# A decoder layer's input projection by Strassen's seven block products, in two sweeps over the contraction

## The chip, the core and the metric

The kernel runs on one core of a Trainium2 chip, as one launch. The metric is the device time of that launch in microseconds; lower is better. Five engines work side by side, each through its own list of instructions in order: TensorE (PE, matrix products), VectorE (DVE), ScalarE (ACT), GpSimd (POOL) and SyncE (SP), which here only issues transfers. They wait for each other by semaphores.

## What is computed

The reference, cut to what matters (S = 1024 positions, model width 2048, 8 heads of 128):

```python
h = jnp.einsum('bsd,de->bse', x, w_in[layer])           # 2048 -> 6144 columns
q, k, v, u_pool, gate = jnp.split(h, [1024, 2048, 3072, 4096], axis=-1)
q, k = rotary_partial(q, positions), rotary_partial(k, positions)   # first 32 of 128
attn = dilated_attention_mixture(q, k, v)               # three strides, one softmax
pooled = [causal_pool_minus_identity(u_groups[g], POOL_WINDOWS[g]) for g in range(4)]
pool_out = einsum(pooled, w_pool[layer]) * pool_scale[layer]
y = concatenate([attn, pool_out]) * silu(gate)
out = jnp.einsum('bse,ed->bsd', y, w_out[layer])
x = layer_norm(DEEPNORM_ALPHA * x + out, ln_gain, ln_bias)
```

The input projection is a product of 1024 x 2048 by 2048 x 6144 in float32.

## The kernel before, in words

**Products.** TensorE takes float32 operands here in a shortened form (F32R). So each operand is split into a high part (a copy by ACT into F32R) and a low part (source minus high part, by DVE): `split`, lines 107 to 109. A product is then three matmuls, high by high, high by low and low by high, summed in PSUM.

**Input projection** (lines 237 to 289). x, transposed, lies split in SBUF for the whole stage: 16 tiles of 128 x 1024 for each part. The 6144 columns are 48 blocks of 128, taken in an order written out in `rounds` (lines 186 to 195): q, k, v and gate of a head, then the next head, at the end the pooling inputs and their gates. Per block the loop runs over 16 contraction tiles; each gives three products by two halves of 512 positions, six matmuls (line 640). The v blocks are computed with positions on the partitions, so that they need no transpose: 12 matmuls of 256 columns per contraction tile (line 633). Weights come in pieces of 128 x 512 (`Pieces`, line 111), three loaded and four split ahead; such a piece holds four contraction tiles of a block.

**Background.** Everything else of the stage (rotation, scores, exponentials, transposes, values, pooling) is cut into steps that wait in a queue, `Background` (line 33). After each block's contraction tile, `bg.tick()` (line 643) adds 0.70 to a credit, 1.0 in the last 12 rounds, and runs a step for each whole credit; so steps are laid into the PE's list between products. `bg.drain(tag)` runs steps at once up to a tag, where a later block needs their buffers. `bg.later` puts off a store by some ticks, so that SP does not stand waiting for it. Rotation (`qk_evac`, line 249) works on the PSUM banks themselves: shuffle and two products, one on DVE and one on POOL (line 265), a sum, then the split. v goes through DRAM once to be read back by residue (`v_d`). Pooling windows (`u_evac`) and their projections (`pool_project`, line 502 the matmul) are background steps too.

**Output projection** (lines 734 to 807). Gated outputs are stored to DRAM (`y_d`), loaded back, split, and multiplied with w_out (`mm3`, line 731), four banks at a time. The first y tiles and weights are loaded and split during the last block of the input projection (lines 613 to 616). Norm and stores of finished rows are background steps again; the last row block is a short tail behind the last matmul.

## Time and profile before

| | us |
|---|---|
| three runs | 1565.33, 1565.43, 1565.63 |
| median | 1565.43 |
| span of the profiled execution (first to last instruction) | 1564.2 |
| PE busy in it | 1551.0 |
| DVE / ACT / POOL busy | 631.6 / 446.2 / 54.6 |
| transfers | 149.75 MB, mean 96 GB/s |

The profiled execution's own time beside its span is not listed; its span lies 1.2 us below the median of the runs. A profile is read here in this order: which engine is busy, which chain of work ended last, what each stage of the span looks like, and last what a single instruction takes. A matmul's own duration overlaps with the next one's, so its cost is the distance of starts.

### The profile page before, as it was taken

To read this page: it belongs to the slowest core of one execution; us is meant where nothing else is said; L and a number is where in the kernel's file an instruction comes from. 1 tells how busy PE (TensorE), PEld (TensorE's weight loads), DVE (VectorE), ACT (ScalarE), POOL (GpSimd) and SP (SyncE) were. 2 spreads that over 40 slices of the span, in tenths; PEclk is the share of its full clock that TensorE was granted. 3 is DMA by queue.
4 is the path that set the end of the run, shared out by engine and by line. 5 is a ranking of instruction groups with operands and counts; after the bars stand their busy time and mean duration, and the time that the engine had idled before them with its cause. 6 is when DMAs were issued, how large, how long until landed. Compare 5 with 4: busy or idle time off the path is not lost.

```text
span 1564.2 us, 20097 instructions
## 1 busy us (share of the span) xinstructions
PE 1551.0 (99%) x8116; PEld 1308.5 (84%) x8116; DVE 631.6 (40%) x1155; ACT 446.2 (29%) x788; POOL 54.6 (3%) x59
## 2 busy tenths in 40 slices
PE   9999999999999999999999999999999999999997
PEld 7898889888899888998888888888888888888886
DVE  4362433233441434424342113454153435476446
ACT  4333232142431323323323113222132424222310
POOL 0010100001000000000000000000000000000001
PEclk9999999999999999999999999999999999999999
DMA  7431213311124111241111222222213557357512
GB/s 239 146 110 34 61 41 89 107 35 41 54 68 128 41 41 54 60 117 57 38 54 54 68 75 84 97 75 61 61 54 114 167 205 242 115 197 242 146 52 104
DMA packets 73085, 149.75 MB, mean 96 GB/s; under 512 B 8288, under 2 KB 12256, under 8 KB 71712
## 3 DMA queue, kind: packets, MB, share of 16 engines
q1 hardware_dynamic: 72704, 148.19, 30.6%
q8 instruction: 63, 1.03, 0.3%
q10 hardware_dynamic: 288, 0.29, 0.1%
q14 instruction: 30, 0.25, 0.1%
HBM read 126.42 MB, written 22.02 MB: 95 GB/s over the span
## 4 chain that ended last, share of the span: by engine, by line
PE 98%; DVE 1%; ACT 1%; issue 0%; DMA 0%; DVEq 0%; SPq 0%
PE mm_ps L640 54%; PE mm_ps L731 10%; PE mm_ps L633 10%; PE s_ps L731 6%; PE o_ps L731 3%; PE t_ps L731 3%; PE s_ps L633 1%; PE s_ps L502 1%; PE s_ps L320 1%; PE o_ps L381 1%; PE o_ps L396 1%; PE s_ps L327 1%; PE o_ps L640 1%; PE o_ps L397 1%; PE t_ps L640 1%; PE t_ps L368 0%
## 5 line engine op out<-in xcount | busy, mean ns | idle before, releaser
L109 DVE TENSOR_TENSOR w_lo<-w_raw,w_hi 128x512 fp32r<-128x512 f32 (+1 forms) x337 | 234.3, 696 | 643.8 <-ACT w_hi L108 643.7
L108 ACT ACTIVATE w_hi<-w_raw 128x512 fp32r<-128x512 f32 (+1 forms) x337 | 212.0, 630 | 806.0 <-PE mm_ps L640 426.3
L640 PE MATMUL mm_ps<-h,w_hi 128*128 128x512 f32 x1248 | 395.9, 398 | 0.0
L640 PE MATMUL mm_ps<-l,w_hi 128*128 128x512 f32 x1248 | 386.1, 391 | 0.0
L640 PE MATMUL mm_ps<-h,w_lo 128*128 128x512 f32 x1248 | 386.0, 390 | 0.0
L640 PEld LDWEIGHTS mm_ps<-h,w_lo 128*128 128x128 f32 x1248 | 234.6, 188 | 50.3
L640 PEld LDWEIGHTS mm_ps<-l,w_hi 128*128 128x128 f32 x1248 | 234.5, 188 | 50.0
L640 PEld LDWEIGHTS mm_ps<-h,w_hi 128*128 128x128 f32 x1248 | 225.6, 188 | 45.7 <-issue 4.0
L633 PE MATMUL mm_ps<-w_hi,h 128*128 128x256 f32 x448 | 128.3, 286 | 0.0
L633 PE MATMUL mm_ps<-w_hi,l 128*128 128x256 f32 x448 | 126.8, 283 | 0.0
L633 PE MATMUL mm_ps<-w_lo,h 128*128 128x256 f32 x448 | 126.7, 283 | 0.0
L633 PEld LDWEIGHTS mm_ps<-w_hi,h 128*128 128x128 f32 x448 | 85.9, 192 | 0.5
L633 PEld LDWEIGHTS mm_ps<-w_lo,h 128*128 128x128 f32 x448 | 85.9, 192 | 0.1
L633 PEld LDWEIGHTS mm_ps<-w_hi,l 128*128 128x128 f32 x448 | 85.8, 192 | 0.0
L731 PE MATMUL mm_ps<-w_hi,h 128*128 128x512 f32 x192 | 74.7, 389 | 0.0
L731 PE MATMUL mm_ps<-w_lo,h 128*128 128x512 f32 x192 | 74.7, 389 | 0.0
L731 PE MATMUL mm_ps<-w_hi,l 128*128 128x512 f32 x192 | 74.7, 389 | 0.0
L731 PE MATMUL s_ps<-w_hi,h 128*128 128x512 f32 x128 | 49.8, 389 | 0.0
L731 PE MATMUL s_ps<-w_lo,h 128*128 128x512 f32 x128 | 49.8, 389 | 0.0
L731 PE MATMUL s_ps<-w_hi,l 128*128 128x512 f32 x128 | 49.8, 389 | 0.0
L342 ACT ACTIVATE p_t<-p_t,nm 128x128 f32<-128x128 f32 (+3 forms) x64 | 35.9, 562 | 32.1 <-DVE nm L335 31.7
L333 DVE CUSTOM_DVE_ANT_0 p_t<-s_ps,mask 128x128 f32<-128x128 f32 (+3 forms) x64 | 31.4, 490 | 28.1 <-PE s_ps L327 25.7
(176 smaller groups left out, 1704.7 us busy)
## 6 DMA issues: line engine op xcount, KB each, us to landing
w_raw<-in_w_in_dram SPq DMA_DIRECT2D x159, 256.0 KB, 2.7
w_raw<-in_w_out_dram SPq DMA_DIRECT2D x112, 256.0 KB, 2.7
w_raw<-in_w_v_dram SPq DMA_DIRECT2D x64, 256.0 KB, 2.7
z<-in_x_n_dram SPq DMA_DIRECT2D x8, 1024.0 KB, 5.1
p_t<-in_x_t_dram SPq DMA_DIRECT2D x15, 512.0 KB, 5.4
out_dram<-z SPq DMA_DIRECT2D x30, 256.0 KB, 3.4
y_d<-p_t SPq DMA_DIRECT2D x8, 512.0 KB, 3.8
y_d<-v_f SPq DMA_DIRECT2D x8, 512.0 KB, 3.5
```

The lines of the kernel that those rows point to most:

```text
L108: ACT.activation(hi, src, AF.Copy)
L109: DVE.tensor_tensor(out=lo, in0=src, in1=hi, op=ALU.subtract)
L320: PE.matmul(s[e][:, n - 2 * P:n], a[:, b * P:b * P + P], k[:, b * P - P:b * P + P], start=j == 0, stop=j == 2)
L327: PE.matmul(s[e][NF * r:NF * r + NF, :width(b) - 2 * P], qf[:, q0:q0 + NF], kv[:, :b - 1, r, :], start=True, stop=True, tile_position=(0, ...
L333: DVE.tensor_tensor_reduce(out=pt, in0=s[e][:, :n], in1=mask[:, NM - n:], op0=ALU.add, op1=ALU.max, scale=1.0, scalar=-3.0e38, accum_out=mx)
L342: ACT.activation(pt, pt, AF.Exp, scale=SCALE, bias=st.pop(("m", m, e)), accum_out=den)
L381: PE.matmul(o[:, 0:2 * P], v[:, 2 * m], p[:, 1:3], start=True, stop=False)
L396: PE.matmul(ov[:, e], v[:, 0, r], far_t[0][:, :, c], start=True, stop=False)
L397: PE.matmul(ov[:, e, 4:6], v[0:64, 1, r], far_t[1][:, :, c], start=False, stop=True)
L633: PE.matmul(o, x[kc][:, ss], y[:, es], start=kc == 0 and n == 0 and b % 2 == 0, stop=kc == KC - 1 and n == 2 and b % 2 == 1)
L640: PE.matmul(t[f], a[:, es], b[kc][:, c], start=kc == 0 and n == 0, stop=kc == KC - 1 and n == 2)
L731: PE.matmul(o, a[:, k % 2, ss], b, start=k == 0 and n == 0, stop=k == KC - 1 and n == 2)
```

## The change

The 48 column blocks are taken in 24 pairs, and the contraction in two sweeps of 1024. In a sweep, positions (two halves of 512), contraction (two quarters of 512) and the two blocks of a pair form 2 x 2 blocks, and the pair's four results come from seven block products in place of eight, with sums and differences of x quarters (made once per sweep, `combo`) and of weight quarters (made per pair on POOL, `combine`) as operands. A block product is 12 matmuls of 512 columns. The first sweep runs over all pairs with no background steps and stores the four results of a pair to DRAM (`q_d`); the second loads them back and adds its own. v now comes out with its columns on the partitions and is transposed by PE (`values`). Rotation works in SBUF. Gates, pooling inputs and window means go through DRAM (`g_d`, `u_d`, `m_d`). The pool projections run after the last pair, and the output projection's buffers are opened after them.

The diff, cut to its core:

```diff
-Q0, K0, U0, G0 = 0, 8, 16, 24
 NF = 32
 NM = 6 * NF + 2 * P
+PAIRS = []
+for _h in range(NH):
+    if _h < 4:
+        PAIRS.append(("u", _h))
+    elif _h in (5, 7):
+        PAIRS.append(("p", (_h - 5) // 2))
+    PAIRS += [("qk", _h), ("vg", _h)]
+PAIRS += [("p", 2), ("p", 3)]
+NP = len(PAIRS)
...
+    def gate(self, key):
+        self.steps.append((None, key))
+    def _blocked(self):
+        while self.steps and self.steps[0][0] is None:
+            if self.steps[0][1] not in self.ready:
+                return True
+            self.steps.popleft()
+        return not self.steps
...
             return
         self.credit += self.rate
-        while self.credit >= 1.0 and self.steps:
+        while self.credit >= 1.0 and not self._blocked():
             self.credit -= 1.0
             self.steps.popleft()[0]()
     def drain(self, tag=None):
...
+        if tag is not None and all(t != tag or f is None for f, t in self.steps):
             return
-        while self.steps:
+        while not self._blocked():
             fn, t = self.steps.popleft()
             fn()
...
+    bg = Background(0.55)
...
+        def cut(self, t):
+            hi = wp.tile([P, 512], F32R, name="w_hi", bufs=3)
+            lo = wp.tile([P, 512], F32R, name="w_lo", bufs=3)
+            split(hi, lo, t)
             self.ready.append((hi, lo))
-            self.made = 1
...
+        def combine(self, n, k):
+            if n >= len(self.order):
+                return
+            r, s = self.raw, self.s
+            a, b, op = {1: (r.get((n, 2)), r.get((n, 3)), ALU.add),
+                        2: (s.get((n, 1)), r.get((n, 0)), ALU.subtract),
+                        3: (r.get((n, 0)), r.get((n, 2)), ALU.subtract),
+                        4: (r.get((n, 1)), s.get((n, 2)), ALU.subtract)}[k]
+            t = wp.tile([P, 512], F32, name="w_sum", bufs=3)
+            POOL.tensor_tensor(out=t, in0=a, in1=b, op=op)
+            s[n, k] = t
...
+                lambda: (self.load(n + 1, 0, 2), self.cut(r[n, 0]), self.combine(n, 2)),
+                lambda: (self.cut(s[n, 2]), self.combine(n, 3)),
+                lambda: self.cut(r[n, 1]),
+                lambda: (self.cut(s[n, 3]), self.load(n + 1, 3, 1)),
+                lambda: (self.cut(s[n, 1]), self.combine(n, 4)),
+                lambda: self.cut(r[n, 3]),
+                lambda: (self.cut(s[n, 4]), self.combine(n + 1, 1)),
+            ]
+        def step(self):
+            if self.steps:
+                self.steps.popleft()()
...
+    def combo(i, src, cuts=1):
+        hi = cp.tile([P, 4, 512], F32R, name=f"ch{i}")
+        lo = cp.tile([P, 4, 512], F32R, name=f"cl{i}")
+        combos[i] = (hi, lo)
+        n = 4 // cuts
+        for c in range(cuts):
+            split(hi[:, c * n:c * n + n], lo[:, c * n:c * n + n], src[:, c * n:c * n + n])
...
+    def product(i, o, first, last):
+        wh, wl = weights.take()
+        xh, xl = combos[i]
+        for kc in range(4):
+            es = slice(kc * P, kc * P + P)
+            for n, (a, b) in enumerate(((wh, xh), (wh, xl), (wl, xh))):
+                PE.matmul(o, a[:, es], b[:, kc], start=first and kc == 0 and n == 0,
+                          stop=kc == 3 and n == 2, skip_group_check=True)
+            if kc == 1:
+                weights.step()
+            bg.tick()
...
+    def quarter():
+        return wp.tile([P, 512], F32, name="q4", bufs=5)
...
+    def store_q(pair, q, t, ticks=2):
+        bg.later(lambda: SP.dma_start(q_d[pair][q], t), ticks)
...
+        a = bank()
+        do(1, a, True)
+        x = temp()
+        ACT.activation(x, a, AF.Copy)
+        b = bank()
+        evac("x", x)
+        do(6, b, True)
+        u2 = temp()
+        add(DVE, u2, x, b)
+        evac("u2", u2)
+        do(2, a, False)
+        evac(0, a, None)
+        do(7, b, False)
+        u3 = temp()
+        add(DVE, u3, x, b)
+        evac("u3", u3)
+        c = bank()
+        do(5, c, True)
+        evac(3, c, u3)
+        do(4, b, False)
+        evac(2, b, x)
+        do(3, c, False)
+        evac(1, c, u2)
+    weights.load(0, 0)
+    x_load(0, 0, 0, cuts=4)
+    weights.load(0, 1)
+    x_load(0, 1, 0, cuts=2)
+    weights.load(0, 2, 3)
...
+    ready = {
+        1: lambda: combo(1, xr[0, 0], 4),
+        2: lambda: combo(2, xr[1, 0], 2),
+        3: lambda: combo(3, xr[1, 1], 2),
+        7: lambda: (x_sum(DVE, "t1", xr[0, 1], xr[0, 0]),
+                    x_sum(POOL, "t3", xr[1, 1], xr[0, 1], xr[0, 1]), combo(7, xr["t3"])),
+        5: lambda: (combo(5, xr["t1"]), x_sum(DVE, "t2", xr[1, 1], xr["t1"])),
+        6: lambda: (combo(6, xr["t2"]), x_sum(DVE, "t4", xr[1, 0], xr["t2"])),
+        4: lambda: combo(4, xr["t4"]),
+    }
+    first_pair(0, ready)
...
+    def sums_out(pair):
+        def evac(q, t, u=None):
+            if isinstance(q, str):
+                return
+            o = quarter()
+            if u is None:
+                ACT.activation(o, t, AF.Copy)
+            else:
+                add(DVE, o, u, t)
+            store_q(pair, q, o)
+        return evac
+    for p in range(1, NP):
+        pair_products(sums_out(p))
...
+    def rotated(which, h):
+        full = heads[which, h][0]
...
+        rot = [None, None]
...
+        def swapped(f):
+            rot[f] = at.tile([64, 512], F32, name="rot", bufs=1)[32:64]
+            DVE.stream_shuffle(rot[f], full[0:32, cols[f]], swap)
+            DVE.tensor_tensor(out=full[0:32, cols[f]], in0=full[0:32, cols[f]], in1=rope[0:32, cols[f]], op=ALU.mult)
+            POOL.tensor_tensor(out=rot[f], in0=rot[f], in1=rope[32:64, cols[f]], op=ALU.mult)
...
+            t = full[0:32, cols[f]]
             DVE.tensor_tensor(out=t, in0=t, in1=rot[f], op=ALU.add)
...
+            ACT.activation(parts["hi"][:, cols[f]], full[:, cols[f]], AF.Copy)
...
+            DVE.tensor_tensor(out=parts["lo"][:, cols[f]], in0=full[:, cols[f]], in1=parts["hi"][:, cols[f]],
+                              op=ALU.subtract)
...
+        return [lambda: swapped(0), lambda: total(0), lambda: (rest(0), swapped(1)), lambda: total(1), lambda: rest(1)]
...
+    def values(h, f, t):
...
+        def by_block():
+            o = ps.tile([P, 4, P], F32, name="t_ps")
+            for b in range(4):
+                PE.transpose(o[:, b], t[:, b * P:b * P + P], ident)
+            ACT.activation(near[:, 4 * f:4 * f + 4], o, AF.Copy)
+        def by_residue():
+            o = ps.tile([P, 4, P], F32, name="t_ps")
+            m = P if f == 0 else 64
+            c = at.tile([P, 4, P], F32, name="pt", bufs=2)
+            ACT.activation(c[:, :, 0:m].rearrange("p r (b u) -> p r b u", u=NF), tv[:, :, 0:m // NF], AF.Copy)
+            for r in range(4):
+                PE.transpose(o[0:m, r], c[:, r, 0:m], ident)
+            ACT.activation(far[0:m, f], o[0:m], AF.Copy)
+        return [by_block, by_residue]
...
+        bg.gate(("v", h))
...
+                bg.add(gate_in)
...
+    def window(c):
...
+            tiles["f"] = at.tile([P, S], F32, name="p_t", bufs=3)
+            SP.dma_start(tiles["f"], u_d[c])
...
+        def turn():
+            u = tiles["u"] = at.tile([P, PAD + S], F32, name="p_t", bufs=3)
+            POOL.memset(u[:, :PAD], 0.0)
+            ACT.activation(folded(u[:, PAD:]), unfolded(tiles["f"]), AF.Copy)
...
+        steps = [fetch, lambda: None, lambda: None, turn, lambda: None]
...
+            o = tiles["old"] or at.tile([P, PAD + S], F32, name="p_t", bufs=3)
...
+            ACT.activation(unfolded(o[:, :S]), folded(tw[:, PAD:]), AF.Copy)
+            bg.later(lambda: SP.dma_start(m_d[c], o[:, :S]), 3)
...
+        tiles = {}
...
+        def fetch():
+            for c in range(2):
+                tiles["m", c] = at.tile([P, S], F32, name="p_t", bufs=3)
+                SP.dma_start(tiles["m", c], m_d[2 * g + c])
+            tiles["w"] = at.tile([P, 512], F32, name="rot", bufs=1)
+            SP.dma_start(tiles["w"], w_pool[g])
...
+        def weights_of():
+            hi = at.tile([P, 512], F32R, name="pt", bufs=2)
+            lo = at.tile([P, 512], F32R, name="pt", bufs=2)
+            split(hi, lo, tiles["w"])
+            tiles["wp"] = (hi, lo)
+        def parts(c):
+            hi = at.tile([P, S], F32R, name="q_hi" if c == 0 else "k_hi")
+            lo = at.tile([P, S], F32R, name="q_lo" if c == 0 else "k_lo")
+            split(hi, lo, tiles["m", c])
+            tiles["c", c] = (hi, lo)
...
+        def gate_in(d):
+            tiles["g", d] = at.tile([P, S], F32, name="p_t", bufs=3)
+            SP.dma_start(tiles["g", d], g_d[NH + 2 * g + d])
...
+            DVE.scalar_tensor_tensor(out=tiles["o", d][:, cs], in0=t, scalar=pscale[:, 2 * g + d:2 * g + d + 1],
+                                     in1=tiles["g", d][:, cs], op0=ALU.mult, op1=ALU.mult)
...
+                bg.later(lambda: SP.dma_start(y_d[NH + 2 * g + d], o), 2)
+        return [fetch, weights_of, lambda: (parts(0), gate_in(0)), lambda: (parts(1), gate_in(1)),
+                lambda: proj(0, 0), lambda: proj(0, 1), lambda: proj(1, 0), lambda: proj(1, 1)]
...
+    def silu_out(t, q, dst):
+        ACT.activation(t, t, AF.Silu)
+        bg.later(lambda: SP.dma_start(dst[:, q * 512:q * 512 + 512], t), 2)
+    def sums_in(pair):
+        kind, i = PAIRS[pair]
+        held = {}
+        def fetch(*qs):
+            for q in qs:
+                held[q] = quarter()
+                SP.dma_start(held[q], q_d[pair][q])
+        def evac(q, t, u=None):
+            if q == "x":
...
+            if q == "u2":
+                fetch(3)
+                add(POOL, held[1], held[1], t)
+                return
+            if q == "u3":
+                add(POOL, held[3], held[3], t)
+                return
+            r, f = q // 2, q % 2
+            cs = slice(f * 512, f * 512 + 512)
+            if kind == "qk":
+                w = "qk"[r]
+                if q == 0:
+                    if i > 0:
+                        bg.drain(("s", i - 1))
+                    for n in "qk":
+                        heads[n, i] = (at.tile([P, S], F32, name=f"{n}_f"),)
+                add(DVE, heads[w, i][0][:, cs], held[q], t)
+                if q == 1:
+                    bg.first(rotated("q", i) + rotated("k", i))
...
+            add(DVE, held[q], held[q], t)
+            if kind == "vg" and r == 0:
+                if q == 0:
+                    if i > 0:
+                        bg.drain(("a", i - 1))
+                    heads["v", i] = (at.tile([P, 8, P], F32, name="v_n"), at.tile([P, 2, 4, P], F32, name="v_f"))
+                bg.first(values(i, f, held[q]))
+                if q == 1:
+                    bg.ready.add(("v", i))
+            elif kind == "vg":
+                silu_out(held[q], f, g_d[i])
+            elif kind == "p":
+                silu_out(held[q], f, g_d[NH + 2 * i + r])
...
+                t = held[q]
+                bg.later(lambda: SP.dma_start(u_d[2 * i + r][:, cs], t), 2)
+                if q == 1:
+                    window(2 * i)
+                    window(2 * i + 1)
+        return evac, fetch
+    for p in range(NP):
+        if p == 1:
+            sa_stack.close()
+            at = at_stack.enter_context(tc.tile_pool(name="at", bufs=1))
...
+        evac, fetch = sums_in(p)
+        fetch(0, 2, 1)
+        pair_products(evac, (lambda i: combo(i, xr[sources[i]])) if p == 0 else None)
+    for g in range(NG):
+        for fn in pool_project(g):
+            bg.add(fn)
+    bg.drain()
+    bg.flush()
+    at_stack.close()
+    proj_stack.close()
...
+    big = ctx.enter_context(tc.tile_pool(name="big", bufs=1))
+    zp = ctx.enter_context(tc.tile_pool(name="zp", bufs=1))
+    sources = [w_out[d, k] for sg in range(2) for d in range(4 - sg) for k in range(KC)]
...
+    def w_load():
+        if place[0] < len(sources):
+            t = zp.tile([P, 512], F32, name="w_raw", bufs=3)
+            SP.dma_start(t, sources[place[0]])
+            raw.append(t)
+            place[0] += 1
+    def w_fill():
+        while place[1] < len(sources) and place[1] - place[2] < 4:
+            t = raw.popleft()
+            hi = zp.tile([P, 512], F32R, name="w_hi", bufs=4)
+            lo = zp.tile([P, 512], F32R, name="w_lo", bufs=4)
+            split(hi, lo, t)
+            ready.append((hi, lo))
+            place[1] += 1
+            w_load()
...
+    for k in range(2):
+        y_load(k, 0)
+        w_load()
+    w_load()
+    y_load(2, 0)
```

A tick now follows every three matmuls of a block product. The host orders x and w_in by these blocks.

## Rows read from the trace of the kernel before

**Rows 1.** The page, part 1 (busy time) and part 4 (chain that ended last)
```profile
PE 1551.0 (99%) x8116; PEld 1308.5 (84%) x8116; DVE 631.6 (40%) x1155; ACT 446.2 (29%) x788; POOL 54.6 (3%) x59
...
PE 98%; DVE 1%; ACT 1%; issue 0%; DMA 0%; DVEq 0%; SPq 0%
```

**Rows 2.** Busy time by stage: us, each engine, granted clock, DMA share, GB/s
```profile
4.60:11.70 7.10, 6.70 (x23) 5.13 (x24) 3.94 (x6) 4.02 (x6) 0.00 (x0) 1.00 0.94 319
...
98.20:850.00 751.80, 751.69 (x4387) 641.17 (x4386) 272.23 (x654) 231.02 (x464) 35.56 (x29) 1.00 0.22 63
850.00:1204.50 354.50, 354.42 (x1566) 291.32 (x1565) 118.40 (x137) 79.81 (x109) 0.78 (x7) 1.00 0.24 74
1204.50:1553.30 348.80, 348.79 (x1584) 290.58 (x1583) 185.30 (x290) 93.71 (x157) 6.17 (x8) 1.00 0.51 167
1553.30:1564.20 10.90, 0.00 (x0) 0.00 (x0) 7.29 (x11) 2.00 (x4) 5.36 (x5) 0.65 0.26 96
```

**Rows 3.** Chain of waits, pieces in order: start us, us, what
```profile
8.27 2.36 PE mm_ps L640 x6
...
671.15 23.23 PE mm_ps L633 x192
694.38 34.03 PE mm_ps L640 x150
...
1335.06 43.52 PE mm_ps L731 x192
```

**Rows 4.** Groups of instructions by line and shape, PE
```profile
L640 PE MATMUL mm_ps<-h,w_hi 128*128 128x512 f32 x1248 | 395.9, 398 | 0.0
...
L633 PE MATMUL mm_ps<-w_hi,h 128*128 128x256 f32 x448 | 128.3, 286 | 0.0
```

**Rows 5.** Instructions in order of time, PE: four transposes (first and last)
```profile
349.74 0.27 PE L355 MATMUL t_ps<-ident,p_t 128*128 128x128 f32 x1
...
350.06 0.27 PE L358 MATMUL t_ps<-ident,p_t 128*128 128x128 f32 x1
```

**Rows 6.** Groups by line and shape, DVE; last row: 98 to 850 us alone
```profile
L109 DVE TENSOR_TENSOR w_lo<-w_raw,w_hi 128x512 fp32r<-128x512 f32 x335 | 233.5, 698 | 640.7 <-ACT w_hi L108 640.7
...
L109 DVE TENSOR_TENSOR l<-p_t,h 128x1024 fp32r<-128x1024 f32 x15 | 18.0, 1224 | 7.9 <-ACT h L108 7.8
...
L260 DVE STREAM_SHUFFLE k_f<-mm_ps 32x512 f32<-32x512 f32 x16 | 11.0, 730 | 0.2
...
L462 DVE TENSOR_TENSOR p_t<-p_t 128x1039 f32<-128x1039 f32 x8 | 9.9, 1238 | 5.0 <-ACT p_t L437 5.0
...
L403 DVE TENSOR_TENSOR p_t<-p_t,gate 128x1024 f32<-128x1024 f32 x8 | 9.8, 1221 | 0.1
...
L109 DVE TENSOR_TENSOR w_lo<-w_raw,w_hi 128x512 fp32r<-128x512 f32 x142 | 99.5, 701 | 298.0 <-ACT w_hi L108 298.0
```

**Rows 7.** Groups by line and shape, ACT
```profile
L108 ACT ACTIVATE w_hi<-w_raw 128x512 fp32r<-128x512 f32 x335 | 211.1, 631 | 805.3 <-PE mm_ps L640 426.3 <-PE o_ps L731 86.7 <-PE mm_ps L633 83.5
...
L108 ACT ACTIVATE h<-p_t 128x1024 fp32r<-128x1024 f32 x15 | 15.5, 1051 | 7.4 <-DMA p_t<-in_x_t_dram 7.3
```

**Rows 8.** Instructions in order of time, 78 to 83 us, DVE and POOL
```profile
78.35 0.69 DVE L109 TENSOR_TENSOR w_lo<-w_raw,w_hi 128x512 fp32r<-128x512 f32 x1 [2.19 <-ACT w_hi L108]
...
79.95 2.53 POOL L265 TENSOR_TENSOR k_f<-k_f,rope 32x512 f32<-32x512 f32 x2 [78.25 <-DVE k_f L260]
...
80.50 1.41 DVE L264 TENSOR_TENSOR mm_ps<-mm_ps,rope 32x512 f32<-32x512 f32 x2
...
81.94 1.10 DVE L109 TENSOR_TENSOR w_lo<-w_raw,w_hi 128x512 fp32r<-128x512 f32 x1
```

**Rows 9.** DMA issues: what, queue, count, size, median us to landing
```profile
w_raw<-in_w_in_dram SPq DMA_DIRECT2D x159, 256.0 KB, 2.7
...
p_t<-in_x_t_dram SPq DMA_DIRECT2D x15, 512.0 KB, 5.4
```

More of the change, by code (lines that the diff above doesn't have):

```diff
@@ L51, in add, with first, _age @@
         self.steps.append((fn, tag))
-    def tick(self):
+    def first(self, fns):
+        for fn in reversed(fns):
+            self.steps.appendleft((fn, None))
+    def gate(self, key):
[6 more added lines that the diff above has]
+        return not self.steps
+    def _age(self):
         for h in self.held:
@@ L57, in tick @@
             self.held.pop(0)[1]()
-        if not self.steps:
+    def tick(self):
+        self._age()
+        if self._blocked():
             self.credit = 0.0
@@ new lines, in pair_products, with do @@
+    def pair_products(evac, before=None):
+        def do(i, o, first):
+            if before is not None:
+                before(i)
+            product(i, o, first, True)
+        a = bank()
+        do(1, a, True)
+        x = temp()
+        ACT.activation(x, a, AF.Copy)
+        b = bank()
[17 more added lines that the diff above has]
+        evac(1, c, u2)
@@ L553 @@
-    pieces.load_first(lambda: x_load(0))
-    for _ in range(2):
-        pieces.load()
-    for kc in range(1, 3):
-        x_load(kc)
-    def constants():
-        SP.dma_start(ident, ident_in)
-        SP.dma_start(rope, rope_in)
-        SP.dma_start(mask, mask_in)
-        SP.dma_start(cor, cor_in)
-        SP.dma_start(pscale, pool_scale)
+            ACT.activation(unfolded(o[:, :S]), folded(tw[:, PAD:]), AF.Copy)
+            bg.later(lambda: SP.dma_start(m_d[c], o[:, :S]), 3)
+        steps.append(mean)
```

544 lines of the change are left out of this document (207 added, 337 removed).

## Prediction

> **What bounds the kernel now.** I read the page first, then the chain of waits, then the busy time by stage, and last the single instructions. The page says that TensorE (PE) is busy 99% of the span, and that the chain that ended last is 98% PE [rows 1]. By stage PE has no hole: from 4.6 us, where the first product starts, to 1553.3 us it is busy all the time, while VectorE (DVE) is at 36% in the attention stage (98 to 850 us) and ScalarE (ACT) at 31% [rows 2]. So the time is the sum of what PE issues. The chain gives its cadence, which is what counts, since one matmul's own duration overlaps the next: 34.03 us for 150 matmuls of 512 columns is 0.227 us each, and 23.23 us for 192 of 256 columns is 0.121 [rows 3]. The input projection is 40 blocks x 16 x 6 = 3840 of the first kind (1248 of each product in one bank name, the other 96 in the first round) and 8 x 16 x 12 = 1536 of the second [rows 4]: 871 + 186 = 1057 us. The output projection takes 348.8 us [rows 2]. The other 143 us of the 1548.7 are attention, pooling and a slow first 12 us (the first matmuls stand 2.36 / 6 = 0.39 us apart [rows 3], though the granted clock reads 1.00, 2.4 GHz, there as everywhere [rows 2]).
>
> **What it removes.** 24 pairs x 2 sweeps x 7 products x 12 matmuls = 4032 of 512 columns, 0.227 us each: 915 us. That they keep this cadence though the stationary side changes at every second matmul is shown by the output projection, which changes it at every one or two: 43.52 / 192 = 0.227 [rows 3]. So PE work falls by 1057 - 915 = **142 us**. This is sure; the rest is what covers are lost.
>
> **What it adds, part by part.**
> - *Transposes of v on PE:* 8 heads x 16 = 128 of 128 columns. Four in a row take (350.06 - 349.74) / 3 = 0.107 us each [rows 5]: +14 us, all on PE. Bounds 12 to 18.
> - *Steady pairs of the first sweep (23):* per pair of 7 x 12 x 0.227 = 19.1 us DVE has 7 splits and 5 sums, 12 x 0.70 = 8.4 us, ACT 7 x 0.63 and two copies, 5.6 us [rows 6, 7], POOL 4 sums of 128x512. No such sum is in the trace; the nearest row is the rope product of the same 512 columns, 2.53 / 2 = 1.27 us [rows 8], so 5 us. The loads and stores are 8 x 256 KB a pair, each landing 2.7 us after issue [rows 9]. All fit below 19.1 us: nothing. The cover is PE itself, with one product (2.7 us) of split weights ahead; without it a split costs 0.63 + 0.70 us per product.
> - *The first pair:* before, x came in 16 pieces and products began with the first. Now 4 MB of x and 1 MB of weights must come for the first pair; at the 319 GB/s of the stretch 4.6 to 11.7 us [rows 2], and the launch before it, the last block is there at about 20 us. Then a chain without cover: t3 on POOL (four times 1.27 = 5.1), the split of 128x2048 (ACT 1.9, DVE 2.3, extended from the 512 and 1024 rows [rows 6, 7]), product 7 done at 32; copy, split of t1 and product 5 at 39; t2, its split and product 6 at 46; t4, its split and product 4 at 52. Against 4.6 + 19.1 and the 3 us that the slow start cost already: **+26**. Bounds 18 (POOL and DVE overlap fully) to 34 (products at the start's 0.39 us).
> - *Start of the second sweep:* the seven splits of 128x2048 sit between products. DVE: 7 x (2.3 + 0.7) + 6 x 0.7 = 25 us against 19.1, and the first split waits for the last sum of the first sweep (3 us): **+8**, bounds 4 to 12.
> - *The second sweep's background:* one tick is now 3 matmuls, 0.68 us, so at a rate of 0.55 a step comes every 1.24 us of PE time; before it was 1.36 / 0.70 = 1.9 us. The rotation of a head is ten steps without PE work, laid into 12.4 us of products. DVE needs for it, per half, shuffle 0.73 [rows 6] and three operations of about 0.69, four halves 11.2 us; the splits and sums that belong to 4.5 products come in between, 4.5 x 1.3 = 5.8; and each half waits for POOL's rope product, 1.27 us [rows 8], of which I take 0.9 as uncovered, 3.6. Sum 20.6 us on a queue in order, against 12.4. The next product's weight split stands behind these steps on DVE, so PE waits for w_lo. One product of lead hides 2.7: 5.5 x 8 heads = **+45**, bounds 10 (DVE runs far enough ahead) to 75 (nothing hidden and POOL's other sums in front of the rope).
> - *Drains:* walking the queue by the order of the code (380 steps on 672 ticks, of which 370 would fit, and gates that stop it while v is not there) gives seven drains with work left, of 5, 3, 8, 20, 8, 3 and 9 steps. Drained steps have no products between them. The one of 20 (last pooling window, then the scores of head 3) is a chain: load 5 us [rows 9], a copy on ACT of 2.1, four shifts of 1.24 [rows 6], a mean of one such and a small operation, 1.4, then masks and exponentials of four score pairs; less its own PE work, 17 us. Four that end in far products and the gating (1.22 [rows 6]) 3.5 each, two short ones 1.5: **+34**, bounds 15 to 55.
> - *Pool projections* now stand at the end, with nothing beside them. The first group waits for its 512 KB loads and for the splits, 8 us; each of the other three for three ACT splits (0.63 + 2 x 1.05) and the DVE split behind them, 3.2 us net: **+20**. Bounds 10 to 40: at the start's slow cadence the 96 matmuls alone would cost 16 us more.
> - *Output projection:* its first y and w wait for the last store's place on SP, 2.7 us of landing [rows 9] and two ACT splits, and then run in with four weight splits ahead of the second y: **+10**, bounds 6 to 16. Before, the last in-projection blocks covered this.
> - *SP and traffic:* 25 MB of sums out and back, and gates and windows; SP issues some 14 transfers per pair at 0.4 us. Nothing, unless a store that waits on DVE stands before the sums' load; then DVE's adds wait, which the range holds.
>
> Sum, against the median of 1565.4 us (the profiled execution, whose own time is not listed, has a span of 1564.2): 1565.4 - 142 + 14 + 26 + 8 + 45 + 34 + 20 + 10 = **1580 us**. All lower bounds give 1500, all upper ones 1670.
>
> **A rule against the change.** While POOL's two rope products ran (79.95 to 82.48 us), a DVE split with both inputs in SBUF took 1.10 us, and 0.69 just before; the DVE products with PSUM operands beside it kept 0.70 [rows 8]. The split ended 0.55 us after POOL did. So a DVE operation with two SBUF inputs waits out a POOL operation here. The Trainium skill, "SBUF — State Buffer", section "Who interferes with whom", states this as an exclusive lock: the second to start is blocked for the whole instruction. By that rule the trace agrees. It is a rival of its own below, since the change takes POOL from 3% to some 40% of the second sweep and moves the rotation's operands from PSUM to SBUF.
>
> **The rivals.**
> - *The cover holds (faster).* Place: the second sweep. DVE has 24 x 9.0 for splits and sums, 8 x 25 for the heads (272.2 us of the attention stage [rows 2] less 99.5 of splits [rows 6], over seven heads), 36 for the windows and 16 for the x splits = 468 us of work there and PE 24 x 19.1 + 8 x 16 = 586, so on the average DVE is free a fifth of the time. If ACT and DVE run ahead through the score steps, where they have slack, the rotation costs its lower bound 10 and the drains 20 in place of 79: 1580 - 49 = **1531**. It decides where rotation and drains together cost less than 64 us. For it: no wait of PE in the trace of before. Against: the lead there was four pieces of 5.4 us, here it is one product of 2.7.
> - *POOL holds DVE up (slower still).* 7 sums of 1.27 us per pair and the rope are 256 us of POOL in about 640. Some 300 two-input DVE operations fall on it with a chance of 0.4 and wait half of 1.27: 77 us of DVE more, 545 in all against PE's 586; then little slack is left, and most of it shows: 1580 + 60 = **1640**.
> - *No change:* the terms cancel, which needs a sum within 3 us of 142.
> - That the products are not fewer is excluded by the count; that they are slower, by the output projection's cadence [rows 3].
>
> **How the numbers follow.** The forecast (1566 to 1625) gets 0.45, POOL's lock 0.13, the faster case 0.37, and no change 0.05; no change is a move of at most 0.2%, 3 us, about what a measurement of this kernel can tell. So faster 0.37, same 0.05, slower 0.58. The likeliest case is the forecast, 1580, though the faster case is near in weight, and its own range is 1566 to 1625. The range for 8 in 10 goes from 1515 (the faster case with the start at its lower bound too) to 1640.
>
> **What would show it.** In the changed kernel's stages: a first sweep of 23 x 19.1 = 438 us with PE full would confirm the cadence; PE below 90% in the second sweep, with PE waiting for w_lo from DVE in the rotation steps, would confirm the main cost; a hole before each of four pool groups and one of 6 us or more before the output projection, the tail terms; 30 us of holes before 55 us, the start. A PE busy share of 95% or more in the second sweep would prove the forecast wrong, and so would a first sweep with holes. DVE splits of over 1 us on the mean would speak for POOL's lock.

## The result, and the profile after

The changed kernel takes **1821.14 us** (median of four runs, 1819.20 to 1824.23); the kernel before takes 1565.53 beside it. The ratio is 1.163, with a 95% interval from 1.162 to 1.165. The forecast, 1580 us with a range to 1640, had the direction right (it gave "slower" 0.58) and the size wrong by 241 us. The profiled execution took 1824.23 us, with a span of 1822.5.

The page, part 1 (busy time) and, from part 2, the granted clock in 40 slices:

```profile
PE 1562.9 (86%) x6896; PEld 1231.6 (68%) x6896; DVE 942.2 (52%) x1528; ACT 569.4 (31%) x984; POOL 467.8 (26%) x330
...
PEclk7799999999987898898977798979898699999999
```

PE issues 1220 matmuls and transposes fewer than before [rows 1], and yet is busy for longer: where the granted clock is low, a product matmul starts 0.43 us after the one before and not 0.227 (counted below). No other engine is near full. Where the time went, by stage (the first sweep's first pair; pairs 1 to 17; 18 to 21; 22 and 23; the second sweep's first pair, 24; pairs 25 to 47; the pooling projections; the output projection), with the columns of [rows 2]:

```profile
0.00:69.70 69.70, 34.99 (x85) 24.01 (x86) 35.16 (x28) 22.00 (x25) 19.84 (x14) 0.71 0.32 109
69.70:393.90 324.20, 324.20 (x1430) 268.46 (x1429) 133.36 (x204) 88.01 (x153) 87.58 (x68) 1.00 0.34 118
393.90:486.20 92.30, 82.12 (x337) 66.19 (x336) 48.36 (x48) 20.70 (x36) 38.66 (x20) 0.94 0.32 113
486.20:524.30 38.10, 38.10 (x169) 31.54 (x169) 15.69 (x24) 12.17 (x19) 10.31 (x8) 1.00 0.33 111
524.30:578.30 54.00, 33.39 (x86) 23.65 (x84) 26.01 (x20) 15.58 (x14) 14.26 (x9) 0.72 0.19 65
578.30:1377.20 798.90, 656.09 (x3117) 502.36 (x3115) 463.90 (x870) 301.76 (x560) 285.60 (x198) 0.89 0.28 95
1377.20:1455.90 78.70, 38.37 (x109) 27.04 (x108) 28.00 (x34) 14.25 (x19) 0.10 (x1) 0.70 0.62 211
1455.90:1822.50 366.60, 355.60 (x1572) 288.40 (x1572) 191.73 (x301) 94.92 (x159) 11.44 (x12) 0.99 0.49 160
```

Pairs 1 to 17 run at 324.2 / 17 = 19.07 us with no hole: seven products in place of eight do what the count says. Everything that was lost lies elsewhere. Against the forecast's own stages:

| stage | forecast | measured | missed |
|---|---|---|---|
| to the end of the first pair | 52 | 69.7 | 18 |
| pairs 1 to 23 | 438 | 454.6 | 17 |
| pair 24, start of the second sweep | 27 | 54.0 | 27 |
| pairs 25 to 47 | 649 | 798.9 | 150 |
| pooling projections, to the output projection | 52 | 78.7 | 27 |
| output projection and end | 360 | 366.6 | 7 |

(The forecast's stages add up to 1578, and 1.2 us lie outside the span. 649 is 23 x 19.05 for the products, 132 for PE's own background work with v's transposes, 45 for the rotation and 34 for the drains; 52 at the end is 22 of matmuls, 20 and 10.) PE's waits, from the waits by engine (us in total, times, longest):

```profile
PE mm L271 <- ACT w_hi L150: 56.7, 26, 9.4
PE s_ps L691 <- ACT q_hi L150: 30.7, 4, 8.3
PE mm L271 <- DVE w_lo L151: 29.7, 23, 2.5
PE o_ps L575 <- ACT p_t L562: 23.0, 3, 8.8
PE mm L271 <- DVE cl L151: 22.8, 10, 2.8
PE s_ps L495 <- DVE mx L508: 15.4, 1, 15.4
PE t_ps L463 <- DVE q L284: 14.5, 9, 2.1
PE t_ps L543 <- ACT pt L536: 12.5, 9, 2.2
```

In pairs 25 to 47 PE stands still for 798.9 - 656.1 = 143 us, and after a hole its clock is low: with the idle time taken off, some 350 of the 1931 distances behind a product matmul are over 0.33 us, most of them 0.43 in place of 0.227. At the full clock's cadence these distances would be less by 519.1 - 1931 x 0.2268 = 81 us. Idle time and lower clock, 143 + 81 = 224, are nearly the whole excess over the products and PE's own background work (some 130 us), 799 - 438 - 130 = 231.

A head's rotation in pair 26, from the timeline (start, us, engine, instruction, idle time before it in brackets):

```profile
609.36 0.61 ACT L150 ACTIVATE w_hi<-w_sum 128x512 fp32r<-128x512 f32 x1
610.01 0.69 DVE L151 TENSOR_TENSOR w_lo<-w_sum,w_hi 128x512 fp32r<-128x512 f32 x1 [2.02 <-ACT w_hi L150]
610.74 0.72 DVE L436 STREAM_SHUFFLE rot<-q_f 32x512 f32<-32x512 f32 x1
611.50 0.68 DVE L437 TENSOR_TENSOR q_f<-q_f,rope 32x512 f32<-32x512 f32 x1
611.59 1.73 POOL L438 TENSOR_TENSOR rot<-rot,rope 32x512 f32<-32x512 f32 x1 [6.10 <-issue]
613.36 0.68 DVE L442 TENSOR_TENSOR q_f<-q_f,rot 32x512 f32<-32x512 f32 x1 [1.18 <-POOL rot L438]
614.07 0.63 ACT L447 ACTIVATE q_hi<-q_f 128x512 fp32r<-128x512 f32 x1 [4.09 <-DVE q_f L442]
614.60 0.58 ACT L341 ACTIVATE u<-mm 128x512 f32<-128x512 f32 x1
615.08 0.62 ACT L150 ACTIVATE w_hi<-w_raw 128x512 fp32r<-128x512 f32 x1
615.73 1.41 DVE L151 TENSOR_TENSOR w_lo<-w_raw,w_hi 128x512 fp32r<-128x512 f32 x1 [1.70 <-ACT w_hi L150]
615.75 0.50 PE L271 MATMUL mm<-ch,w_hi 128*128 128x512 f32 x1 [2.40 <-ACT w_hi L150]
```

Read downwards: w_lo, shuffle, product and sum on DVE, the high-part copy on ACT behind the sum, and only then the next weight's split on ACT. From one w_hi to the next are 5.7 us, and 6.5 to the one after (621.61), where a product lasts 2.7.

### The profile page after: what moved, and what is told of

The parts are those of the page before. It is cut to its first block, busy times and chain, and to the rows that moved or that the text cites. A ratio compares the mean times of both kernels' runs of the same rounds, so it can differ in the third digit from the quotient of the medians.

```text
span 1822.5 us, 19496 instructions
## 1 busy us (share of the span) xinstructions
PE 1562.9 (86%) x6896; PEld 1231.6 (68%) x6896; DVE 942.2 (52%) x1528; ACT 569.4 (31%) x984; POOL 467.8 (26%) x330
## 5 line engine op out<-in xcount | busy, mean ns | idle before, releaser
L271 PE MATMUL mm<-ch,w_hi 128*128 128x512 f32 x1332 | 563.1, 423 | 68.6 <-ACT w_hi L150 56.7
L271 PE MATMUL mm<-ch,w_lo 128*128 128x512 f32 x1332 | 551.0, 414 | 29.8 <-DVE w_lo L151 29.7
L271 PE MATMUL mm<-cl,w_hi 128*128 128x512 f32 x1332 | 546.0, 410 | 22.8 <-DVE cl L151 22.8
L271 PEld LDWEIGHTS mm<-ch,w_hi 128*128 128x128 f32 x1332 | 265.8, 200 | 137.4 <-ACT w_hi L150 69.7
L151 DVE TENSOR_TENSOR w_lo<-w_raw,w_hi 128x512 fp32r<-128x512 f32 x256 | 214.0, 837 | 258.3 <-ACT w_hi L150 258.2
L271 PEld LDWEIGHTS mm<-ch,w_lo 128*128 128x128 f32 x1332 | 265.6, 199 | 105.6 <-DVE w_lo L151 48.5
L271 PEld LDWEIGHTS mm<-cl,w_hi 128*128 128x128 f32 x1332 | 266.1, 200 | 78.3 <-DVE cl L151 27.6
L150 ACT ACTIVATE w_hi<-w_raw 128x512 fp32r<-128x512 f32 x256 | 160.5, 627 | 269.0 <-PE mm L912 88.7
L151 DVE TENSOR_TENSOR w_lo<-w_sum,w_hi 128x512 fp32r<-128x512 f32 x192 | 147.0, 765 | 122.9 <-ACT w_hi L150 122.8
L196 POOL TENSOR_TENSOR w_sum<-w_raw 128x512 f32<-128x512 f32 x96 | 133.7, 1392 | 125.7 <-DVE w_lo L151 110.0
```

What stands on the lines that cost most here:

```text
L150: ACT.activation(hi, src, AF.Copy)
L151: DVE.tensor_tensor(out=lo, in0=src, in1=hi, op=ALU.subtract)
L196: POOL.tensor_tensor(out=t, in0=a, in1=b, op=op)
L271: PE.matmul(o, a[:, es], b[:, kc], start=first and kc == 0 and n == 0, stop=kc == 3 and n == 2, skip_group_check=True)
```

## The experiments

The kernel before took 1565.3 to 1567.5 us beside them. "Pairs 25 to 47" is always the stretch from the first matmul of pair 25 to the last of pair 47, 799 us in the changed kernel; "v/gate pairs" are eight among them (26, 29, 32, 35, 37, 40, 42, 45), 333 us there, in which a head's rotation falls. Each experiment is a single run. In the changed kernel and the three runs that edit other stages alone (the start of the second sweep, the end, the address), pairs 25 to 47 took 795, 795, 799 and 802 us; so a difference of less than some 7 us there tells nothing.

**Is it the lead of one product?** The forecast's mechanism. One weight is split ahead at the start, and each later one comes a product earlier.

```diff
     first_pair(0, ready)
+    weights.step()
```

> One more weight split made ahead (two products of lead in place of one), nothing else. Theory A (the background's steps stand ahead of the next weight split on ACT and DVE, and one product of lead is too short): most waits of PE for w_hi and w_lo in the second sweep (67 us of idle time there) go, the clock drops less often, and the stretch of pairs 25 to 47 falls from 799 us by 60 us or more, so the kernel comes to 1760 us or less. Theory B (POOL's sums hold DVE up by the port, so DVE is simply full): a longer lead moves the waits and saves under 20 us. Pairs 18 to 21 of the first sweep, which wait for POOL's x sums of 4.5 us, should also fall from 23 us towards 21 by A.

1808.9 us. Pairs 18 to 21 fell from 92.4 to 76.2 us, all that was lost there. Pairs 25 to 47 took 801: nothing. PE waits no longer for the weights there but, in the same engines' queues, for the next things in them (39.4 us for v's last sum, where it was 14.5, and 39.7 in the drains, where it was 23.0). The lead is not what the second sweep lacks.

**Is it POOL's answer?** The rope product is given to DVE, so that the sum waits for nobody.

```diff
-            POOL.tensor_tensor(out=rot[f], in0=rot[f], in1=rope[32:64, cols[f]], op=ALU.mult)
+            DVE.tensor_tensor(out=rot[f], in0=rot[f], in1=rope[32:64, cols[f]], op=ALU.mult)
```

> The rope product of the rotated half (32 of them) on DVE in place of POOL. Theory A (DVE waits for POOL's answer in the middle of each rotation step): per half the 1.2 us of idle DVE before the rotation's sum goes and 0.7 us of DVE work comes; the eight pairs of v and gate, 333 us in all, fall by 25 to 60 us. Theory B (POOL's sums hold DVE up): 32 operations of 1.7 us less on POOL, but 32 more on DVE, a change of less than 15 us.

1820.0 us, pairs 25 to 47 at 795 and the v/gate pairs at 331: no change beyond the spread. The sum no longer waits for POOL, and DVE has 0.7 us more to do per half; that the second took what the first gave is likely, but not shown.

**Background and POOL apart.** One kernel leaves rotation, attention, v's transposes and windows of the second sweep out; the other keeps them and leaves POOL's sums of that sweep out.

> Rotation, attention, v's transposes and the windows are left out of the second sweep (gates are still loaded, multiplied and stored, pool projections read the pooling inputs). Theory A: without background steps the second sweep runs at 19.05 us a pair like the first, in spite of POOL's 7 sums a pair: 23 pairs in 440 us. Theory B (port): POOL's three more sums a pair than in the first sweep already cost the products something: 21 us a pair or more, 480 us.

> In the second sweep POOL's sums are left out (weight sums replaced by single quarters, the three sums with the kept results left out); POOL keeps only the rope products. Theory B (port): DVE's weight splits come back from 0.8 to 0.70 us and pairs 25 to 47 lose most of their 233 us over the ideal, 100 us or more. Theory A (queue order and lead): the waits for ACT and DVE stay, since rotation and drains stay; the stretch loses under 60 us.

Without the background 1462.2 us, and pairs 25 to 47 without a hole (the row of that stretch, columns as in [rows 2]):

```profile
575.00:1016.00 441.00, 441.00 (x1933) 361.36 (x1931) 240.16 (x306) 125.47 (x214) 230.59 (x158) 1.00 0.46 152
```

So products, weight sums, stored sums and traffic of the second sweep cost nothing beyond 23 x 19.05 = 438 us, POOL's 230 us of sums among them. Without POOL's sums but with the background 1785.7 us:

```profile
574.00:1338.00 764.00, 635.92 (x3117) 490.78 (x3115) 415.11 (x870) 301.51 (x560) 57.83 (x39) 0.91 0.29 99
```

The stretch took 764 us: beside the background these sums cost 35. DVE's 870 instructions took 463.9 us with them and 415.1 without.

**Is it the bank that is read and written again?** Each product gets its own bank, first alone and then with the longer lead; the sums are taken outside PSUM.

```diff
-        do(2, a, False)
-        evac(0, a, None)
...
+        c = bank()
+        do(2, c, True)
+        evac(0, c, x)
```

> Every block product of a pair starts in a bank of its own; the sums that were made by accumulating on a bank already read once (u2 to u3, x to c11 and so on) are made by DVE, one operation more a pair, and by one more sum on POOL. Theory D (a product that accumulates waits until ACT or DVE, queued behind background steps, has read the bank's first content; the cover is the one product between): with weights still one product ahead, waits of PE for w_hi and w_lo remain, and pairs 25 to 47 fall from 799 us by 20 to 60 us. Theory C (DVE and ACT are simply too full or too long in chains): no fall, or a rise by the added work.

> Both: own banks, and weight splits two products ahead. Theory D: the two covers were each limiting alone, so together pairs 25 to 47 fall by 100 us or more from 799 and PE's waits in the rotation steps nearly go. Theory C: the fall is under 40 us, since the rotation's chain through DVE, POOL and ACT takes its time whatever the lead.

1847.4 and 1822.3 us, pairs 25 to 47 at 820 and 815: no fall, but a rise, with one more sum on DVE in each pair. This theory falls.

**The rotation left out** (q and k are split unrotated):

> The rotation is left out of the second sweep (q and k are only split into high and low parts; shuffle, two products and sum go). It sizes the rotation's term, predicted as 45 us: the eight pairs of v and gate, 333 us against 8 x 24 ideal, fall by 45 us by the prediction; by theory D, which puts most of these pairs' excess on the chain through DVE, POOL and ACT, by 80 us or more.

1704.6 us; pairs 25 to 47 took 683, the v/gate pairs 213 in place of 333, and the other fifteen pairs 470 in place of 466. The rotation costs **116 us**, all of it in the v/gate pairs, where the forecast had 45.

**The start of the second sweep.** Its x splits are issued behind the first sweep's last seven products; the output projection's one-column constant also moved.

```diff
-        pair_products(evac, (lambda i: combo(i, xr[sources[i]])) if p == 0 else None)
+        pair_products(evac)
...
+        pair_products(sums_out(p), (lambda i: combo(i, xr[sources[i]])) if p == NP - 1 else None)
```

> Two edits in other stages. The second sweep's x splits are issued one by one behind the products of the first sweep's last pair in place of ahead of the products of the second sweep's first: that pair's 54 us fall to 20 to 30. And the one-column tile half is allocated behind the output projection's split tiles and not ahead of them: if the 0.233 us cadence there (0.227 before) comes from where its tiles lie in SBUF, the stretch from the end of the pool projections falls by 6 to 7 us; if not, it stays.

1795.6 us. Pair 24 fell from 54.0 to 21.7 and pair 23 rose from 19.0 to 27.2: 24 us gained. The output projection became some 9 us shorter too, see the last run.

**Is it the order on ACT?** The timeline above suggests a ring: sum, high-part copy, next split. Here the copy runs one step later.

```diff
-        return [lambda: swapped(0), lambda: total(0), lambda: (rest(0), swapped(1)), lambda: total(1), lambda: rest(1)]
+        return [lambda: swapped(0), lambda: total(0), lambda: (high(0), swapped(1)), lambda: (rest(0), total(1)),
+                lambda: high(1), lambda: rest(1)]
```

> Changed kernel, but the high-part copy of a rotated head on ScalarE runs one rotation step behind VectorE's sum instead of right behind it; the rotations of q and of k share two steps, so that a pair still has ten. Theory of the ring (the high-part copy waits for VectorE's sum and stands ahead of the next weight split's high half on ScalarE, whose low half stands ahead of the next swap on VectorE, so that each product waits for a ring of some 6.5 us): pairs 25 to 47 fall from 799 us by 60 us or more, those with v or the gate from 333 us to 270 or less, the kernel from 1821 to some 1750 to 1760. Rival (VectorE and ScalarE simply have too much work for these products, in whatever order): pairs 25 to 47 change by less than 20 us.

1816.6 us, pairs 25 to 47 at 791, the v/gate pairs at 326. The fall of 8 us is hardly more than the spread, where the theory of the ring wanted 60. The ring that I had read from the timeline is not the cause: a chain that is plain to see in one place is not yet what bounds the stage.

**The end.** Weight fetched first, gates fetched into free buffers, the next group's fetches ahead of this group's matmuls.

> Changed kernel, but in the four pooling projections at the end the weight is fetched ahead of the two pooled operands, the gate is fetched into the buffers of v's two halves instead of the ring of p_t, and the next group's fetches are issued before this group's projections. If the wait for the fetched weight is what makes a group 16.7 us, the stretch from the last product to the first matmul of the output projection falls from 79 us to 50 to 60, and the kernel to some 1795 to 1800. If the split on ScalarE and VectorE of the fetched operands is what lasts, it falls by less than 8 us.

1803.2 us; from the last product to where the output projection runs without a hole 61 us in place of 79 (to its first matmul 55 in place of 73), and the wait for the weight is out of the chain. The chain of the changed kernel shows what was removed, three times in a row: SP's issue, which waits for the group before, then the fetch, two splits, and the matmuls.

```profile
1389.60 0.76 DVE q_f L692
1391.23 0.78 SPq L661
1392.06 6.26 DMA rot<-in_w_pool_dram
1398.96 1.05 ACT q_hi L150
1400.03 1.24 DVE q_lo L151
1401.32 4.63 PE s_ps L691 x11
```

**Drains.** The background's rate goes from 0.55 to 0.75.

> Changed kernel with the background's rate of steps raised from 0.55 to 0.75, so that less of it is left for the drain behind the last v tile (pair 36, 54.4 us). If what is left to drain is what costs, pair 36 falls to 40 us or less and pairs 25 to 47 together by 10 us or more. If each background step costs the same wherever it stands, pair 36 falls and the pairs ahead of it rise by as much: 799 us within 8.

1818.5 us, pairs 25 to 47 at 794. Pair 36 fell from 54.4 to 34.6, and the others rose by 15; the difference of 5 lies within the spread. The steps that moved cost about the same beside products as in the drain: the products were no cover for them. That does not hold for every step: pairs 28, 31, 39 and 44 have background steps, scores above all, and no hole of PE.

**All repairs together:**

> Changed kernel with every repair in one: the weight split two products ahead, the second sweep's x splits issued behind the first sweep's last products, the high-part copy one step behind the sum, the pooling projections' fetches ahead, the constant of the output projection allocated behind its tiles, and the splits of the first pair's sums in four cuts. If the losses add up, about 16 (x sums of pairs 18 to 21), 26 (start of the second sweep), 60 to 70 (rotation), 20 (end), 9 (output projection) and 5 to 10 us (first pair) go, which gives some 1670 to 1690 us, still above the kernel before. If the rotation's share is work and not order, some 1735 to 1750.

1739.1 us. The stages add up, but pairs 25 to 47 stayed at 795. PE's first two waits in it were for v's last sum, in front of the transposes, and in the drains:

```profile
PE t_ps L471 <- DVE q L284: 42.8, 12, 6.4
PE o_ps L583 <- ACT p_t L570: 35.5, 3, 11.9
```

**Dependences or occupied engines?** The rotation's instructions run at the same steps on a scratch tile that nobody waits for, once with POOL's product and once without; q and k stay unrotated.

```diff
-            DVE.stream_shuffle(rot[f], full[0:32, cols[f]], swap)
+            DVE.stream_shuffle(scd[0:32], rope[0:32, cols[f]], swap)
...
-            POOL.tensor_tensor(out=rot[f], in0=rot[f], in1=rope[32:64, cols[f]], op=ALU.mult)
+            POOL.tensor_tensor(out=scd[32:64], in0=rope[32:64, cols[f]], in1=rope[32:64, cols[f]], op=ALU.mult)
```

> Changed kernel in which the rotation's instructions (per half head a shuffle, a product and a sum on VectorE and a product on GpSimd) run at the same steps on a scratch tile from the rope table, so that q and k aren't rotated and neither VectorE waits for GpSimd nor ScalarE's high-part copy for the sum. If the rotation costs through who waits for whom, pairs 25 to 47 stay near the 683 us of the kernel without the rotation (at most 710). If it costs through the time that its instructions occupy VectorE and GpSimd, ahead of what TensorE needs, they come back to some 780 to 800 us.

> As the kernel with the rotation's instructions on a scratch tile, but GpSimd's product left out too (the rotation isn't computed). If VectorE's three instructions alone carry the cost, pairs 25 to 47 are within 15 us of that kernel. If it's GpSimd's product, beside which VectorE runs slower or stands, they are within 20 us of 683.

1769.7 and 1764.3 us. The stretch of pairs 25 to 47 without rotation, with DVE's part on scratch, and with POOL's too (one row of each kernel, columns as above):

```profile
574.90:1258.00 683.10, 610.76 (x3117) 477.71 (x3115) 399.19 (x742) 299.76 (x560) 228.76 (x166) 0.95 0.33 111
```
```profile
577.10:1315.70 738.60, 629.07 (x3117) 488.38 (x3115) 462.88 (x870) 299.68 (x560) 234.40 (x166) 0.93 0.30 102
```
```profile
575.70:1320.90 745.20, 630.84 (x3117) 489.55 (x3115) 471.57 (x870) 299.62 (x560) 275.80 (x198) 0.92 0.30 101
```

Neither extreme holds. DVE gets 63.7 us more work and the stretch grows by 55.5: nearly all of it shows, though DVE is busy only 463 / 739 = 63%. POOL's product adds 7, no more than the spread, and the dependences the last 799 - 745 = 54. How those 54 divide among the sum's wait for POOL, the copy's wait for the sum and the rest stays open; the two single repairs gave 4 and 8, which the spread hardly lets one tell from nothing.

**Are PE's waits separate, or one that moves on?** All repairs, and v's transposes three steps later.

```diff
-                bg.first(values(i, f, held[q]))
+                bg.first([lambda: None] * 3 + values(i, f, held[q]))
```

> Kernel with every repair (1739 us), and the transposes of v three background steps later, so that they stand no more right behind the product whose sum they read: TensorE waited 42.8 us there for VectorE's sum. If that wait is a loss of its own, pairs 25 to 47 fall from 795 us by 30 or more. If TensorE then waits at the next thing that stands behind VectorE's queue, they fall by less than 12 us.

1710.6 us, the fastest complete form tried, 145 us above the kernel before. Pairs 25 to 47 fell to 765, by 30, which is just the bound that I had set. So this wait is in the main a loss of its own; some of its 42.8 us moved on, as the drains' wait grew from 35.5 to 47.6 us.

**The address in the output projection:**

```diff
-    half = zp.tile([P, 1], F32, name="half")
...
+                half = zp.tile([P, 1], F32, name="half")
```

> Changed kernel with one thing moved: the one-column constant of the output projection is allocated behind the projection's other tiles instead of ahead of them, which shifts their addresses by 4 bytes. If that address is what made a matmul of the output projection 0.2333 us instead of 0.2267, their cadence is 0.2267 and the kernel some 8 to 9 us faster than 1821; if the faster cadence of the kernel with early splits came from its other edit, the cadence stays 0.2333 and the time within 3 us.

1809.6 us. Its longest chain pieces, 192 matmuls each, changed kernel first and this one second:

```profile
1498.65 44.80 PE mm L912 x192
```
```profile
1491.68 43.52 PE mm L912 x192
```

44.80 / 192 = 0.2333 us became 0.2267, which the kernel before had too [rows 3]; the projection, from its first matmul to its last, fell from 361.2 to 352.3 us. (The rest of the 11.6 us by which this run lies below the median is no more than the spread of the earlier stages.) In all five kernels on record with the tile behind, the kernel before among them, the cadence is 0.227, and in all thirteen with it ahead 0.233. The edit also issues the tile's memset later; that this one instruction would slow every matmul of the stage is unlikely, but it was not moved by itself.

## Why the prediction was wrong

The step that failed is the cover in the second sweep: what a background step costs beside the products, and which wait of PE it causes. Of the 150 us missed in pairs 25 to 47, 71 are the rotation's (116 measured, 45 forecast) and some 81 the rest of the background's (115 against the drains' 34). The other terms missed by less, each by a step of its own.

- **Removed products, -142: right.** Pairs 1 to 17 run at the forecast's cadence, and so does the whole second sweep without its background (441 us for 438).
- **"Steady pairs of the first sweep: nothing": wrong by 17 us.** The text counted POOL's four sums of 128x512 per pair and passed over the four x sums of 128x2048 that POOL makes in pairs 18 to 21. From the timeline of pair 18:

```profile
405.48 4.56 POOL L262 TENSOR_TENSOR x_r<-x_r 128x2048 f32<-128x2048 f32 x1
405.56 5.02 DVE L151 TENSOR_TENSOR w_lo<-w_raw,w_hi 128x512 fp32r<-128x512 f32 x1
410.64 0.50 PE L271 MATMUL mm<-ch,w_lo 128*128 128x512 f32 x1 [2.55 <-DVE w_lo L151]
```

A split of 0.69 us takes 5.02: POOL's sum started 0.08 us before it and ended 0.54 us ahead of it. The three other sums show the same. The effect was in [rows 8] and in the forecast, which priced it as an average over the second sweep only. The longest single operation, 4.6 us against a lead of 2.7, is what decides. The second product of lead in the first experiment covers it in full (76.2 us for four pairs). The Trainium skill, "SBUF — State Buffer", section "Who interferes with whom", says that a VectorE instruction with two SBUF inputs contends with a GpSimd instruction that reads SBUF, by an exclusive lock. By that rule the trace agrees.
- **The first pair, +26: 43 us.** Two things were left out. DVE was taken as free for t1, but the splits of the second and third x blocks stand there first, so that POOL's t3 starts at 28.57 and not at 20; and after the wait that follows, of 7.6 us, the clock is low (0.71 in the stage), so that product 7 is done at 42.5 and not at 32. The three products behind it took 27 us and not 20, most of their matmuls 0.43 us apart. Splits in four cuts brought the first pair from 60.3 to 51.1 us in the kernel with all repairs.
- **Start of the second sweep, +8: 35 us.** The sum counted DVE's 25 us against 19.1. But each product needs its own split of 128x2048, high and low, right before it, and nothing runs ahead; so ACT's and DVE's times stood in a row, PE stopped for 20.6 us, and in between most of its matmuls stood 0.43 us apart. Issued beside the first sweep's last pair, the same splits cost 8 us on pair 23 and 3 on pair 24.
- **The rotation, +45: 116 us. Here the mechanism failed, and not only the size.** "PE waits for w_lo" and "One product of lead hides 2.7" predict that a second product of lead helps; it gave nothing. In the changed kernel PE waited more for w_hi, from ACT (56.7 us), than for w_lo, from DVE (29.7). The background's instructions and the products' splits and sums share DVE's and ACT's lists. Of what the rotation adds to DVE, nearly all comes out as time, and its dependences add as much again. The forecast's queue arithmetic had DVE as the one engine that counts, at 20.6 us for a head against 12.4; it had neither ACT's waits nor what a late DVE delays besides w_lo (v's transposes, the evacuations), nor the clock: leaving the rotation out gave back 70 us of PE's idle time (142.8 against 72.3), but also 35 us of products at the lower clock. Rotation and drains are not two separate terms either. Where a v/gate pair drains the head before, the rest of the new head's rotation stands first in the queue and runs with no product beside it; in pairs 35, 37 and 42 ACT's copy of an attention result then stands behind a high-part copy that waits for DVE's sum. PE's wait for that copy, 23.0 us in the changed kernel, is nearly gone without the rotation:

```profile
PE o_ps L571 <- ACT p_t L558: 1.4, 3, 0.5
```

- **Drains, +34, too small.** Without the rotation pairs 25 to 47 still take 683 - 438 - 130 = 115 us more than PE's work: 72 us in which PE stands still, and the lower clock behind them. What each part of the background has in it is known only in part. Pair 36, with the drain that was sized at 17 us, takes 54.4, some 28 more than a quiet pair like 25 or 47 with its own background. v's transposes, priced at PE's 14 us, wait for DVE's sum as well, which was priced at nothing: 14.5 us in the changed kernel, 42.8 once the lead is longer.
- **The end, +20 and +10: 57 in all**, by the fetches: 5.3 to 6.8 us in each of four groups, of which the forecast had the first.
- **The rival "POOL holds DVE up", 1640:** beside the background POOL's sums cost 35 us, not 60. They add 49 us to DVE's busy time, not 77, and the mean weight split in pairs 25 to 47 took 0.89 us with them and 0.70 without, not over 1. It is a part, not the bound.

The rival "the cover holds" fell; its argument was the mean (DVE free a fifth of the time). DVE was busy 464 of 799 us, and the kernel was slower all the same: a share of busy time says nothing of what waits in a list behind what.

The forecast named a PE share below 90% in the second sweep as its sign, and it came: 656 / 799 = 82%. It named holes in the first sweep as proof against it, and they came too.

## What to carry to other kernels

When the products between two background steps get shorter, recount the lists of all engines that feed them, not the mean load of one: cover is what a list in order lets run ahead, and a step that waits stops everything behind it. Price a hole of PE above its length, since matmuls behind it run at the lower clock: here 143 us of holes came with 81 us of that. Where a GpSimd operation holds up a VectorE one, look at the longest single operation against the lead, not at the average.

## What was not expected of the hardware

- One tile of 4 bytes per partition, allocated ahead of the moving operands in SBUF, made a matmul of 512 columns 0.2333 us in place of 0.2267 (3%), 8.9 us over the output projection. The step in which the address counts was not looked for.
- After holes most product matmuls start 0.43 us apart. In the start of the second sweep, where PE was busy for 33.4 of 54.0 us, the granted clock was 0.72, and in the pooling projections, 38.4 of 78.7, it was 0.70. Both lie between the two levels, 1.2 and 2.4 GHz, so part of each stage ran at the lower one.
- A VectorE subtraction of 128x512, 0.69 us by itself, lasted 5.02 us beside one GpSimd operation of 4.56.
